# The mixers' list scheduler prices VectorE, ScalarE and GpSimd instructions from a profile

## Chip, cores and metric

One core of a Trainium2 chip. The metric is the device time of one execution in microseconds (us), the median of several runs. Engines: PE is TensorE, DVE VectorE, ACT ScalarE, POOL GpSimd, SP the queue that issues most transfers.

## What is computed

One layer of a diffusion transformer block on 256 latent and 256 context tokens of width 1024: modulation vectors, an input projection, two sequence mixers (a diagonal state space "S5" over both directions and a chunked state space "SSD" over both directions), a gated merge, and a mixture of 32 experts of which each token takes 4.

```python
proj_lat = u_lat @ p['w_in']
s5_l, xbc_l, dt_l, z_l, ga_l, gb_l = jnp.split(proj_lat, IN_SPLITS, axis=-1)
...
ya_l, ya_c = s5_mixer(s5_c, s5_l, p, with_ctx_out)
yb_l, yb_c = ssd_mixer(xbc_c, dt_c, z_c, xbc_l, dt_l, z_l, p, with_ctx_out)
...
merged = (sigmoid(ga) * (ya @ w_branch_a) + sigmoid(gb) * (yb @ w_branch_b)) @ w_out
h_lat = h_lat + g_m * merged
h_lat = h_lat + g_f * moe_ffn(rms_norm(h_lat, norm_ffn_w) * (1 + sc_f) + sh_f, p)
return rms_norm(h_lat, final_norm_w)
```

All weights are float32. The expert weights alone are 32 x 3 matrices of 1024 x 1024, 402.7 MB.

## The kernel before, in words

The program has four stages. A front (modulation vectors, the tokens' norm and their split into a high and a low float32r part, small tables), the mixers, the merge (`glu`, `wa`, `wb`, `wo`, 16 weight tiles or more each, with `column` and `split`), and the experts (`moe`), whose weights stream in 384 tiles of 1 MB (`mw`, issued in `Loads.until`, L1856) into 12 and later 17 buffers. The first 12 of them sit in memory that the mixers' front pools give back (`front.close()` after `mixers()`); they are issued during the merge, and the other 5 buffers come with the experts.

The change touches the mixers alone. `mixers()` does not write its instructions in one fixed order. It has some fifteen Python generators, one for each strand of work, which yield before every step the engine that it needs and what it waits for:

- `gemm`: the input projection. For each block of 512 weights a tile `w` is loaded, ACT casts it to the high part `h`, DVE or POOL subtracts to get the low part (also `h`), and PE multiplies (`mm`). 144 such blocks, four load buffers, two PSUM banks.
- `conv`: five-tap convolution of a column, `cv`: one ACT instruction and four SCALAR_TENSOR_TENSORs on DVE, then a Silu. The last tap frees the PSUM bank for `gemm`.
- `decays`, `prep`, `ssd`: for each of 8 groups the SSD scan. `decays` loads `rt` (16 times, one buffer, freed by the last `yps` product of the decay before), DVE makes `et` from it (8 TENSOR_SCALARs), ACT takes exponentials, POOL multiplies `rt`, and `ssd` multiplies `et` by `xl` (two TENSOR_TENSORs), accumulates `yps` on PE, and ends a group with `mb`, a norm (`zt` squared on ACT, summed on PE, square root `rs` on ACT, reciprocal and `dg` on DVE, spread by PE), and `ybT`.
- `vgen`, `tables`, `states`, `outputs`: the S5 scan. `vgen` makes `V`, `tables` makes `T` on POOL, `states` makes `rot`, `Y` and `l4a`; `outputs` makes 16 weight blocks `Wt` (the generator `gen`), passes each through PE and ACT twice into `strip`, writes four strips to DRAM and reads them back as `Toe` in 2 x 8 transfers.
- `sigmoids`: the last 16 columns of the projection (the gates), which share the two PSUM banks of `gemm`.

`Plan` (L1331 on) then plays a list scheduler: it keeps a clock for each engine, at each step takes the generator that can start first, and among those on the same engine within 260 ns of it the one with the best rank (`PRIO`, `PACE`). A clock is moved by the instruction's price, which `Planned.cost` gives (L1446 on). The prices therefore set the order in which the instructions are written, and with it, after the framework's own placement, the order of each engine's queue. `gemm` also looks at the clocks: a low part goes to DVE where `plan.clock["dve"] + 600 < plan.clock["pool"] + 1200`, else to POOL. Every planned instruction is recorded in one line, L1442, so that the trace is read by tile names.

Of the kernel before, what the change touches and what calls it, by code (L numbers as in the profile page):

```python
# [1407 lines left out]
def key(x):  # L1408
    return getattr(x, "tensor", x).name


class Planned:
# [33 lines left out]
    def cost(self, op, args, kw, out, ins, n):  # L1446
        plan, name = self.plan, self.name
        if name == "pe":
            wide = ins[0]
            m = math.prod(wide.shape[1:])  # L1450
            part = 0.25 if m <= 32 else 0.5 if m <= 64 else 1
            if op == "transpose":
                return 109 * wide.shape[0] / P
            return max(n, 16) * (4 if ins[1].dtype == F32 else 1) * 0.42 * part
        if name == "act":
            f = next((a for a in args if isinstance(a, AF)), None)
            table = plan.SETS.get(f, plan.table)
            switch, plan.table = 1280 * (table != plan.table), table
            return 60 + 0.85 * n + switch
        if name == "pool":  # L1460
            return 80 + 2.2 * n
        if op == "tensor_tensor_scan":
            return 63 + 2.1 * n
        if op == "reciprocal":
            return 63 + 6.3 * n
        fast = op in ("tensor_copy", "tensor_scalar") and not any(key(a) in plan.psum for a in (out, *ins))
        return 63 + (0.52 if fast else 1.05) * n


class Shared:  # L1470
# [476 lines left out]
```

## Time and profile before

| | us |
|---|---|
| runs: median (lowest, highest) | 1853.15 (1849.97, 1854.26) |
| the profiled execution, its own time | 1846.35 |
| its span, first to last instruction | 1844.2 |
| busy in the span: PE, DVE, ACT, POOL | 1589.1, 904.5, 506.8, 290.0 |

The profiled execution has 2.15 us outside its span. Busy time of an engine is an average over stages with different limits, so the stages are read one by one: a view by windows gives each engine's busy time in a stretch; the view of waits says what an engine stood idle for; the timeline lists an engine's instructions with their start, length and, in brackets, the idle time before them and what ended it.

### The profile page before, as it was taken

Reading aid. Unit: us, or ns where it says so; the run is one execution under the profiler, and the core shown is the slowest. Engines: PE = TensorE matmul, PEld = TensorE weight load, DVE = VectorE, ACT = ScalarE, POOL = GpSimd, SP = SyncE. Lnnn points to the kernel's source line nnn. Section 1 sums busy time; section 2 is a strip of 40 time slices with the busy share of each in tenths; the row PEclk is TensorE's granted clock in tenths of the full one; section 3 lists DMA queues with packets and bytes.
Section 4 is the critical chain, followed back from the end, with each engine's and each line's share of the span. In section 5 each row is a group of like instructions: output and inputs, shape, how many; then the busy total and the mean of one; then the engine's idle time right before and its main releaser. Section 6 shows DMA issues by size and latency. Waiting matters only on the chain. (4 is left out here: it accounts for less than half of the span.)

```text
span 1844.2 us, 27968 instructions
## 1 busy us (share of the span) xinstructions
PE 1589.1 (86%) x11118; PEld 935.1 (51%) x11118; DVE 904.5 (49%) x1671; ACT 506.8 (27%) x893; POOL 290.0 (16%) x297
## 2 busy tenths in 40 slices
PE   6798888976988799897998888898888889988987
PEld 3576666764766698783533232333333444333443
DVE  7668899888898546664222222242222223212233
ACT  5333453552435565342111111111111111111111
POOL 5133445435331330100000000000000000000000
PEclk8899898987997999998999999999999999988998
DMA  8677554444542357784999999999998999999984
GB/s 309 181 236 237 178 144 136 119 121 110 148 127 64 114 155 264 235 281 161 417 418 417 417 418 417 413 418 417 418 410 350 418 417 418 418 417 419 418 349 174
DMA packets 141415, 539.36 MB, mean 292 GB/s; under 512 B 31736, under 2 KB 44952, under 8 KB 91920
## 3 DMA queue, kind: packets, MB, share of 16 engines
q1 hardware_dynamic: 136032, 526.95, 75.7%
q10 hardware_dynamic: 4608, 7.95, 1.3%
q8 instruction: 143, 2.34, 0.5%
q0 software_dynamic: 560, 1.52, 0.3%
q14 instruction: 72, 0.59, 0.1%
HBM read 529.60 MB, written 6.77 MB: 291 GB/s over the span
## 5 line engine op out<-in xcount | busy, mean ns | idle before, releaser
L1519 PE MATMUL p_gu<-mw,xe 128*64 128x512 f32 x2048 | 474.8, 601 | 45.2 <-DMA mw<-in_mu 28.4
L1442 PE MATMUL mm<-uh,h 128*128 128x256 f32 (+1 forms) x1152 | 323.6, 361 | 45.2 <-DVE cv L1442 29.9
L1519 PEld LDWEIGHTS p_gu<-mw,xe 128*64 128x64 f32 x2048 | 174.2, 137 | 335.7 <-issue 176.8
L1442 PEld LDWEIGHTS mm<-uh,h 128*128 128x128 f32 x1152 | 209.6, 201 | 85.4 <-issue 42.3
L1629 PE MATMUL p_y<-mw,aT 128*64 128x512 f32 x1024 | 243.4, 627 | 3.4 <-issue 3.4
L1442 PE MATMUL mm<-ul,h 128*128 128x256 f32 (+1 forms) x576 | 202.5, 352 | 0.0
L1442 POOL TENSOR_TENSOR h<-w,h 128x512 fp32r<-128x512 f32 x99 | 150.3, 1522 | 279.3 <-ACT h L1442 213.6
L1637 DVE SCALAR_TENSOR_TENSOR yw<-p_y,gs,xq 64x512 f32<-64x512 f32 x64 | 48.0, 750 | 287.3 <-PE p_y L1629 286.2
L1629 PEld LDWEIGHTS p_y<-mw,aT 128*64 128x64 f32 x1024 | 75.3, 144 | 147.4 <-issue 144.0
L1442 ACT CAST h<-w 128x512 fp32r<-128x512 f32 x144 | 88.1, 618 | 168.7 <-PE mm L1442 121.2
L1442 PEld LDWEIGHTS mm<-ul,h 128*128 128x128 f32 x576 | 116.0, 201 | 13.5 <-issue 3.1
L1533 DVE TENSOR_SCALAR au<-p_gu 128x512 f32<-128x512 f32 x32 | 22.1, 692 | 198.7 <-PE p_gu L1519 198.7
L1639 ACT CAST yh<-yw 64x512 fp32r<-64x512 f32 x64 | 39.4, 616 | 285.4 <-DVE yw L1637 285.4
L1527 DVE TENSOR_SCALAR ag<-p_gu 128x512 f32<-128x512 f32 (+1 forms) x34 | 23.0, 676 | 169.8 <-PE p_gu L1519 169.8
L1442 DVE SCALAR_TENSOR_TENSOR cv<-mm,cw,cv 128x508 f32<-128x508 f32 (+3 forms) x128 | 85.6, 673 | 11.0 <-ACT cv L1442 10.6
L359 DVE TENSOR_TENSOR low<-w,hi 128x512 fp32r<-128x512 f32 x80 | 59.6, 751 | 41.6 <-ACT hi L357 40.3
L1528 ACT ACTIVATE as<-ag 128x512 f32<-128x512 f32 (+1 forms) x34 | 21.0, 617 | 210.5 <-DVE ag L1527 210.5
L1442 ACT ACT_TABLE_LOAD x55 | 70.6, 1283 | 29.9 <-DVE cv L1442 29.1
L357 ACT CAST hi<-w 128x512 fp32r<-128x512 f32 x80 | 49.4, 620 | 70.3 <-PE mm L349 24.8
L1613 PE MATMUL p_t<-ident,au 128*128 128x128 f32 x128 | 30.5, 325 | 39.7 <-PEq L1730 25.2
L1442 DVE TENSOR_SCALAR et<-rt,acs,lnd 128x128 f32<-128x128 f32 x128 | 45.9, 413 | 23.6 <-DMA rt<-acd 23.4
L1442 DVE TENSOR_TENSOR h<-w,h 128x512 fp32r<-128x512 f32 x45 | 39.2, 872 | 31.8 <-ACT h L1442 31.8
(452 smaller groups left out, 2335.2 us busy)
## 6 DMA issues: line engine op xcount, KB each, us to landing
mw<-in_mg SPq DMA_DIRECT2D x128, 1024.0 KB
mw<-in_mu SPq DMA_DIRECT2D x128, 1024.0 KB
mw<-in_md SPq DMA_DIRECT2D x128, 1024.0 KB
w<-in_wg SPq DMA_DIRECT2D x96, 256.0 KB
ada<-in_ada SPq DMA_DIRECT2D x32, 256.0 KB
Toe<-in_ada SPq DMA_DIRECT2D x16, 512.0 KB
vT<-Ed SPq DMA_DIRECT2D x16, 512.0 KB
l8a<-in_ada SPq DMA_DIRECT2D x16, 512.0 KB
```

The source lines that it names most:

```text
L357: act.copy(hi, w)
L359: lo.tensor_tensor(low, w, hi.bitcast(F32), op=ALU.subtract)
L1442: return fn(*args, **kw)
L1519: mm = pe.matmul(dst[c * q:c * q + c, 0:n], lhs(k), w[:, o:o + n], start=(i == 2 and k == 0), stop=(k == KD - 1))
L1527: dve.tensor_scalar(g_, pg, 7.0, None, op0=ALU.min)
L1528: sg = act.activation(s_, g_, AF.Sigmoid, scale=1.702)
L1533: dve.tensor_scalar(u_, pu, -7.0, 7.0, op0=ALU.max, op1=ALU.min)
L1613: pe.transpose(pa[:, q * P:(q + 1) * P], u_[:, q * P:(q + 1) * P], ident)
L1629: self.done = pe.matmul(py[64 * q:64 * q + 64], aT[:, k % 4, k // 4], wts[e, 2, c // load.unit][:, c % load.unit:c % load.unit + 512], sta ...
L1637: dve.scalar_tensor_tensor(w[rows], self.py[rows], self.gs[rows, nh, j:j + 1], gf[rows, 512 * nh:512 * nh + 512], op0=ALU.mult, op1=ALU.mult)
L1639: act.copy(self.hi[rows, nh], w[rows])
```

## The change

New prices in `Planned.cost`: a larger fixed part for all three engines, a larger still one on ScalarE where the scale is a tile, forms of VectorE instruction told apart (TENSOR_SCALAR, SCALAR_TENSOR_TENSOR, the rest), and a factor of 1.2 for other VectorE instructions of which no operand is in PSUM. TensorE's prices, the ranks and all other constants stay.

```diff
@@ -1456,15 +1456,20 @@
             f = next((a for a in args if isinstance(a, AF)), None)
             table = plan.SETS.get(f, plan.table)
             switch, plan.table = 1280 * (table != plan.table), table
-            return 60 + 0.85 * n + switch
+            return (330 if hasattr(kw.get("scale"), "shape") else 150) + 0.89 * n + switch
         if name == "pool":
-            return 80 + 2.2 * n
+            return 300 + 2.3 * n
         if op == "tensor_tensor_scan":
-            return 63 + 2.1 * n
+            return 115 + 2.1 * n
         if op == "reciprocal":
-            return 63 + 6.3 * n
-        fast = op in ("tensor_copy", "tensor_scalar") and not any(key(a) in plan.psum for a in (out, *ins))
-        return 63 + (0.52 if fast else 1.05) * n
+            return 145 + 6.3 * n
+        if op == "tensor_scalar":
+            return 280 + 0.48 * n
+        if op == "scalar_tensor_tensor":
+            return 200 + 1.06 * n
+
+        shared = not any(key(a) in plan.psum for a in (out, *ins))
+        return (145 + 1.04 * n) * (1.2 if shared else 1)
```

The instructions of the mixers stay the same but for two low parts, which go from POOL to DVE (99 and 45 before, 97 and 47 now), and two more table loads on ACT (66, now 68 in the program). Their order moves almost from the mixers' start. Three places of it:

DVE, the end of the second of the eight groups of the SSD scan: `mb`, its product with `zt`, the reciprocal `rs`, `dg` and the first `ybT`. Before, from that product to the reciprocal:

```order
L1442 TENSOR_TENSOR mb<-mb,zt 128x512
L1442 SCALAR_TENSOR_TENSOR strip<-id_551,d_127,strip 128x16
L1442 TENSOR_TENSOR vtv<-V,vT 128x512
L1442 SCALAR_TENSOR_TENSOR cv_2704<-mm,cw,cv_2704 128x2x254
L1442 TENSOR_TENSOR vT<-V,vT 128x4x128
L1442 SCALAR_TENSOR_TENSOR cv_2704<-mm,cw,cv_2704 128x2x255
L1442 TENSOR_TENSOR h<-w,h 128x512
L1442 SCALAR_TENSOR_TENSOR cv_2704<-mm,cw,cv_2704 128x2x255
L1442 RECIPROCAL rs<-rs 128x2
```

Now, from the last `mb` to `ybT`:

```order
L1442 SCALAR_TENSOR_TENSOR mb<-cv_1983,ssdd,yps 128x256
L1442 TENSOR_TENSOR bt<-bt,aux 128x2x256
L1442 TENSOR_TENSOR mb<-mb,zt 128x512
L1442 RECIPROCAL rs<-rs 128x2
L1442 TENSOR_TENSOR dg<-ident,rs 128x256
L1442 TENSOR_TENSOR vtv<-V,vT 128x512
L1442 SCALAR_TENSOR_TENSOR ybT<-mb,ssdn,aux 128x256
```

Work that stood between the product, the reciprocal and `ybT` has gone from there: the reciprocal follows the product at once, and between `dg` and the first `ybT` one instruction is left.

SP, the last strip of S5 (its write to DRAM and its 2 x 8 reads `Toe`) and the last loads of `rt` for the decays. Before:

```order
L1442 DMA rt<-acd 128x1024
L1442 DMA w<-in_wgate 128x512 x5
L1442 DMA strip_5733<-strip 4x128x240
L1442 DMA rt<-acd 128x1024
L1442 DMA w<-in_wgate 128x512
L1442 DMA Toe<-strip_5733 16x8x128 x8
L1442 DMA w<-in_wgate 128x512 x3
L1442 DMA rt<-acd 128x1024
L1442 DMA Toe<-strip_5733 16x8x128 x8
```

Now:

```order
L1442 DMA w<-in_wgate 128x512 x8
L1442 DMA rt<-acd 128x1024 x2
L1442 DMA strip_5810<-strip 4x128x240
L1442 DMA Toe<-strip_5810 16x8x128 x8
L1442 DMA rt<-acd 128x1024
L1442 DMA w<-in_wgate 128x512 x2
L1442 DMA Toe<-strip_5810 16x8x128 x8
```

The last `rt` but one has moved ahead of the strip's write, and the last `rt` stands behind the first eight `Toe`.

DVE, the same end of the mixers: the last strip (TENSOR_TENSOR and SCALAR_TENSOR_TENSOR `strip`) and the last decay but one (`et<-rt` x8 and its products `et<-et,xl`). Before:

```order
L1442 TENSOR_TENSOR h<-w,h 128x512
L1442 TENSOR_TENSOR strip<-strip,w_6188 128x16
L1442 SCALAR_TENSOR_TENSOR strip<-id_551,d_127,strip 128x16
L1442 TENSOR_TENSOR xw_6165<-aux,wend 128x512
L1442 SCALAR_TENSOR_TENSOR mb<-cv_5204,ssdd,yps 128x256
L1442 TENSOR_TENSOR bt<-bt,wend 128x2x256
L1442 SCALAR_TENSOR_TENSOR mb<-cv_5266,ssdd,yps 128x256
L1442 TENSOR_TENSOR bt<-bt,aux 128x2x256
L1442 TENSOR_TENSOR mb<-mb,zt 128x512
L1442 TENSOR_TENSOR h<-w,h 128x512
L1442 TENSOR_SCALAR et<-rt,acs,lnd 128x128 x8
L1442 RECIPROCAL rs<-rs 128x2
```

Now:

```order
L1442 TENSOR_TENSOR mb<-mb,zt 128x512
L1442 TENSOR_TENSOR strip<-strip,w_6359 128x16
L1442 TENSOR_SCALAR et<-rt,acs,lnd 128x128 x8
L1442 SCALAR_TENSOR_TENSOR strip<-id_551,d_127,strip 128x16
L1442 RECIPROCAL rs<-rs 128x2
L1442 TENSOR_TENSOR dg<-ident,rs 128x256
L1442 SCALAR_TENSOR_TENSOR ybT<-mb,ssdn,aux 128x256 x2
L1442 TENSOR_TENSOR et<-et,xl 128x4x128 x2
L1442 TENSOR_TENSOR h<-w,h 128x512 x2
L1442 TENSOR_SCALAR et<-rt,acs,lnd 128x128 x8
```

The last instruction of the last strip now stands behind the eight TENSOR_SCALARs of the last decay but one; before, it stood ahead of them by seven instructions.

## Rows read from the trace of the kernel before

**Rows 1.** The page's 40 slices: share of the DMA engines, and GB/s.
```profile
DMA  8677554444542357784999999999998999999984
GB/s 309 181 236 237 178 144 136 119 121 110 148 127 64 114 155 264 235 281 161 417 418 417 417 418 417 413 418 417 418 410 350 418 417 418 418 417 419 418 349 174
```
**Rows 2.** Issues of the expert weights, from the view of the tile mw.
```profile
L1856 SPq DMA_DIRECT2D mw<-in_mg x128: 327/328/2254, 689.5 to 1776.8; - x128
L1856 SPq DMA_DIRECT2D mw<-in_md x128: 327/328/1332, 787.1 to 1797.7; - x128
```
**Rows 3.** Busy time by windows: us, then PE, PEld, DVE, ACT, POOL, PEclk, DMA, GB/s.
```profile
96.00:606.70 510.70, 430.06 (x4031) 337.38 (x4029) 439.95 (x812) 219.73 (x355) 215.31 (x206) 0.90 0.50 145
606.70:652.20 45.50, 33.69 (x334) 29.03 (x330) 21.31 (x44) 25.37 (x36) 12.49 (x7) 0.89 0.38 110
652.20:684.20 32.00, 32.00 (x294) 31.93 (x293) 11.80 (x17) 20.70 (x39) 14.51 (x12) 1.00 0.62 185
684.20:845.00 160.80, 138.19 (x1054) 130.58 (x1053) 106.60 (x203) 74.91 (x145) 11.51 (x5) 0.95 0.71 238
845.00:1844.00 999.00, 886.13 (x4843) 362.15 (x4840) 257.29 (x410) 121.94 (x235) 2.59 (x2) 0.96 0.96 393
```
**Rows 4.** Waits of DVE from 96 to 606.7 us: total, times, longest.
```profile
DVE cv L1442 <- ACT cv L1442: 10.6, 5, 4.1
DVE strip L1442 <- ACT strip L1442: 9.9, 4, 5.5
DVE et L1442 <- DMA rt<-acd: 9.6, 4, 5.5
DVE rot L1442 <- PE s L1442: 7.4, 4, 2.9
...
DVE ybT L1442 <- PE aux L1442: 1.9, 1, 1.9
```
**Rows 5.** Timeline of DVE, 606 to 652 us: start, length, what, [idle before].
```profile
606.10 0.68 DVE L1442 TENSOR_TENSOR et<-et,xl 128x512 f32<-128x512 f32 x1
...
610.41 0.47 DVE L1442 SCALAR_TENSOR_TENSOR mb<-cv,ssdd,yps 128x256 f32<-128x256 f32 x1
...
620.21 2.14 DVE L1442 TENSOR_SCALAR et<-rt,acs,lnd 128x128 f32<-128x128 f32 x8 [4.81 <-DMA rt<-acd]
...
627.77 3.06 DVE L1442 TENSOR_TENSOR et<-et,xl 128x512 f32<-128x512 f32 x2
...
636.76 2.14 DVE L1442 TENSOR_SCALAR et<-rt,acs,lnd 128x128 f32<-128x128 f32 x8 [5.34 <-DMA rt<-acd]
...
649.85 0.17 DVE L1442 RECIPROCAL rs<-rs 128x2 f32<-128x2 f32 x1 [2.65 <-ACT rs L1442]
...
651.27 0.87 DVE L1442 SCALAR_TENSOR_TENSOR ybT<-mb,ssdn,aux 128x256 f32<-128x256 f32 x2 [0.79 <-PE aux L1442]
```
**Rows 6.** Timeline of SP's queue, 609 to 638 us.
```profile
609.47 0.56 SPq L1442 DMA_DIRECT2D strip<-strip  x1
610.13 2.15 SPq L1442 DMA_DIRECT2D rt<-acd  x1
614.25 0.33 SPq L1442 DMA_DIRECT2D w<-in_wgate  x1
618.97 5.05 SPq L1442 DMA_DIRECT2D Toe<-strip  x8
...
633.03 0.33 SPq L1442 DMA_DIRECT2D rt<-acd  x1
```
**Rows 7.** DVE by line and form, 45 to 652 us: count, busy, mean ns, idle before.
```profile
L1442 DVE TENSOR_TENSOR V<-V,vT 128x512 f32<-128x512 f32 x48 | 42.9, 914 | 0.1
...
L1442 DVE TENSOR_TENSOR et<-et,xl 128x512 f32<-128x512 f32 x32 | 30.5, 972 | 1.6 <-ACT et L1442 1.5
L1442 DVE TENSOR_TENSOR h<-w,h 128x512 fp32r<-128x512 f32 x34 | 30.3, 893 | 14.4 <-ACT h L1442 14.4
```
**Rows 8.** The same instructions as minimum, median and maximum ns.
```profile
L1442 DVE TENSOR_TENSOR V<-V,vT x48: 661/684/2869, 98.0 to 524.5; 128x512 f32<-128x512 f32 x48
```

## The prediction

> **What bounds the kernel now.** I start with the 40 slices [rows 1]. From slice 20 on the DMA engines are full, at 417 or 418 GB/s but for a few slices; before that they are half idle. The full part is the expert weights: 402.7 MB at 418 GB/s are 963 us. Next, when they may start [rows 2]: the first tile is issued at 689.5 us, after the mixers, and the last at 1797.7. Until the experts begin at about 845 us only 12 tiles of 1 MB fit. So the end of the kernel is the end of the mixers plus a stretch that the change does not touch: whatever the mixers lose or gain arrives at the end in full, one to one.
>
> The windows [rows 3] divide the rest. From 96 to 606.7 us, 510.7 us, DVE is busy for 440.0, POOL for 215.3, ACT for 219.7. PE shows 430.1, but its overlapping matmuls are counted with modelled ends and it waits inside its blocks. DVE is the engine that sets the pace there, with 70.7 us idle. The waits [rows 4] split that idle time over many causes, none above 10.6 us. From 606.7 to 652.2 us DVE is busy for 21.3 of 45.5 us: a serial chain, the last two decays [rows 5]. Each waits for its load of `rt`, which waits for the decay before. From 652.2 to 684.2 PE is busy throughout: the gate columns, which cannot be shortened by an order. So the new order can act on 70.7 us of idle in the middle, on the chain of 45.5 us, and on how long DVE's own instructions take.
>
> **The change, part by part.** It adds no work and removes none. A table load more or less on ACT lies beside DVE's work and costs nothing while ACT is busy for 43% of the middle; without that cover the two new ones would cost a few us. Two low parts pass from POOL to DVE at 0.893 us each [rows 7]. What counts is how much DVE work stands ahead of a fixed point: with each form's mean duration, the work up to the products of the 14th decay is 0.8 us more than before. **+0.8 us.**
>
> *The end chain.* Call T0 the end of those products, 606.78 us now [rows 5]. The next `mb`, which waits for the decay's matmuls, starts 3.6 us later; the `rt` load for the 15th decay is issued at T0 + 3.4 [rows 6], but its TENSOR_SCALARs start only at T0 + 13.4. The `rt` load after it takes 3.7 us (633.03 to 636.76, rows 5 and 6). The difference is the strip's write, issued just ahead: `Toe`, which needs it, is not issued until 9.5 us after it [rows 6]. In the new order this `rt` stands ahead of the write, so the data are there at T0 + 7.1, and some 7.5 us of DVE work are written ahead of the TENSOR_SCALARs: they start at T0 + 7.5 and gain 6 us. Then SP takes most of it back. The strip's last DVE instruction follows the TENSOR_SCALARs (2.1 us), so its write is issued at T0 + 9.9; eight `Toe` wait 9.5 us for it and take 5.05 us to issue; only behind them comes the last `rt`, at T0 + 24.4. Now it is issued at T0 + 26.2. From there to the end of the last `ybT` it is 19.1 us (633.03 to 652.14) in both. So the chain ends at T0 + 43.5 instead of 45.4: **-1.9 us**, between -6 (the strip's write is no longer in the way) and +6 (the strip comes 8 us later, when ACT or PE holds it up).
>
> *`rt` in the middle.* 9.6 us in four waits, the longest 5.5 behind another strip [rows 4]. A decay needs 3.4 us of matmuls and 3.7 us of load after the one before, 7.1 in sum. In the new order four of the earlier decays have 6.7 to 8.2 us of DVE work in between, enough or nearly; one still has its load behind a strip. I keep 5.5 us for that one: **-4.1 us**, bounds -9.6 and +5.
>
> *`strip` in the middle.* DVE waits 9.9 us for ACT's copies [rows 4], 5.5 at once. Between the last `Wt` of a block and its `strip` the new order leaves less than 5 us once before T0 (before: twice), so the short ones are hardly fewer; but the longest wait had 30 us of DVE work in between and came from PE's queue standing still. Such an accident may go or come again. I take **-4 us**, bounds -9.9 and +5.
>
> *The end of a group.* This speaks against the change. The reciprocal needs ACT's square, PE's sum and ACT's root; at the very end, with nothing in between, that wait is 2.65 us, and `ybT` then waits 0.79 [rows 5]. In the middle there is so far one wait, 1.9 us for `ybT` [rows 4], because other work stands in between. In the new order the second group has none before the reciprocal, and of the first six groups one has nothing and four have one instruction between `dg` and `ybT`. With a latency of 1.35 us, half way between 0.79 and 1.9, and 0.68 us for one instruction: 1.35 + 4 x 0.7 + 2.65 - 1.9 = **+4.9 us**, bounds 0 and +19 (the last group's 3.44 us in six groups, less 1.9).
>
> *Sum:* 0.8 - 1.9 - 4.1 - 4.0 + 4.9 = -4.3 us. Against the profiled execution, 1846.35 us, that is 1842.0. That execution is 6.8 us faster than the median of the runs, 1853.15, against which the changed kernel will be read: 1848.9.
>
> *What the new prices assume, against the row.* The change multiplies all VectorE instructions without a PSUM operand by 1.2. The rows do not show a factor: `V` has a median of 684 ns and a maximum of 2869 [rows 8], with a mean of 914 [rows 7]; most instances are not stretched at all. The Trainium skill ("SBUF — State Buffer", Who interferes with whom) says that GpSimd and a VectorE instruction with two SBUF inputs exclude each other for a whole instruction and do not share; by that rule, the trace agrees, no constant factor can be right for any one instruction, and the stretch depends on which two instructions meet. Over the median of 684 ns, `V`, `et<-et` and `h` lose 48 x 0.230 + 32 x 0.288 + 34 x 0.209 = 27.3 us [rows 7]. In the sum I leave this unchanged, because POOL does the same work less two low parts.
>
> **Rivals.**
> 1. *The other waits fall too.* Of the 70.7 us idle, 21.4 are in the three terms above (9.6, 9.9, 1.9); 49.3 are for `cv`, `rot` and others [rows 4]. The prices are nearer to the rows than before (a `V` was priced 600 ns, now 813), so a consumer should less often be written ahead of its data. If these fall by the 40% that I took for `rt` and `strip`, that is another -19.7: 1829 us. Against it: PE's prices, whose queue caused the longest waits, are unchanged.
> 2. *The waits only change places.* The order moves, the idle time stays near 70 us; this is also the case in which the prices hardly act because the framework places the instructions. 1853 us. The DVE orders differ from the first S5 block on, which speaks against the second half.
> 3. *The end of the groups decides.* If each of six groups waits like the last one now, 3.44 us, the term is +18.7 instead of +4.9: 1848.9 + 13.8 = 1862.7. The other terms give -9.2; the kernel becomes slower than before once a group waits (9.2 + 1.9) / 6 = 1.85 us on average. For it: PE works through its queue in order and may be inside a block of the projection. Against it: but for the second, the groups before the seventh keep three to seven rows between product and reciprocal.
> 4. *More meetings of DVE and POOL.* If the stretch of 27.3 us grows by a third, +9: 1858 us. A third less is as easily had, since the order decides who meets whom; I give the growth the chance because nothing in the change avoids a meeting. The Trainium skill ("SBUF — State Buffer", Who interferes with whom) has issue order decide which of the two blocks, which fits both signs.
>
> **Numbers.** Forecast 1848.9 us, chance 0.36, with 1842 to 1856 as its own range. Rival 1: 0.22. Rival 2: 0.14. Rival 3: 0.16. Rival 4: 0.12. 0.2% is 3.7 us, about what a measurement can tell from no change. Faster by more than that: rival 1 and somewhat over half of the forecast's range, 0.22 + 0.22 = 0.44. The same: the rest of the forecast but 0.02, rival 2 and a little of rival 4, 0.12 + 0.14 + 0.02 = 0.28. Slower: 0.16 + 0.10 + 0.02 = 0.28. The range from 1832 to 1863 leaves out half of rival 1, the far end of rival 3, and little else.
>
> **What would show it.** In the profile after, the first weight tile should be issued some 4 us before 689.5 us less any offset at the start, and the experts' stretch should be as long as now. DVE's `rt` wait before the 15th decay should be near zero and that before the 16th remain at 5 us or more; the strip's write should be issued after that decay's TENSOR_SCALARs. The waits of `rs` and `ybT` in the middle should be near 7 us in sum. I am wrong in kind if the experts' stretch takes up or gives back what the mixers did, if DVE's busy time moves by more than 5 us at equal work (then the meetings with POOL decide), or if DVE waits mostly for PE's queue in places that I have not named.

## The result, and the profile after

The changed kernel is slower: 1901.8 us (1897.4 to 1905.8, 4 runs) against 1853.4 for the kernel before, a ratio of 1.027 [1.024, 1.030], some 48 us. The forecast was 1848.9, with a range from 1832 to 1863. The profiled execution took 1902.17 us, with a span of 1900.1. It lies at the median of its runs, while that of the kernel before lies some 7 us under its median, so the two spans differ by 55.9 us where the medians differ by 48.

The view by windows, as [rows 3]. Its first two cuts are at the same events (the end of the products of the 14th decay, 657.96, and the last `ybT`, 707.6); the third is at the first expert tile, 742.9, where [rows 3] cut 5.3 us ahead of that tile. Columns us, PE, PEld, DVE, ACT, POOL, PEclk, DMA, GB/s:

```profile
96.00:657.96 561.96, 442.03 (x4036) 349.46 (x4038) 438.76 (x811) 230.51 (x365) 222.60 (x207) 0.87 0.47 135
657.96:707.60 49.64, 36.84 (x340) 31.62 (x337) 25.96 (x48) 20.10 (x31) 12.24 (x6) 0.69 0.30 85
707.60:742.90 35.30, 35.30 (x331) 34.82 (x331) 13.23 (x23) 22.92 (x43) 13.20 (x11) 1.00 0.52 165
742.90:900.00 157.10, 131.12 (x1006) 123.36 (x1005) 102.58 (x194) 71.28 (x137) 11.50 (x5) 0.96 0.72 239
900.00:1899.00 999.00, 884.67 (x4846) 357.87 (x4843) 257.59 (x411) 122.23 (x236) 2.58 (x2) 0.96 0.96 393
```

The first weights of the tile `mw`, as in [rows 2]:

```profile
L1861 SPq DMA_DIRECT2D mw<-in_mg x128: 327/328/2058, 742.9 to 1832.7; - x128
```

The experts' last 999 us have the same DMA share as before, 0.96, and the same 393 GB/s. The first tile is issued 53.4 us later (689.5 to 742.9), and from there to the end of the span it is 2.5 us more (1154.7, now 1157.2). So the loss arose in the mixers: 51.2 us up to T0, the end of the products of the 14th decay (606.78 before, 657.96 now), 4.3 in the end chain, and 2.1 less from the last `ybT` to the first tile. The windows of DVE up to T0 say what kind of time it is. The kernel before and then the changed one; columns as above, DVE alone:

```profile
45.00:606.78 561.78, 476.04 (x889) 0.89 0.51 148
```
```profile
45.00:657.96 612.96, 477.31 (x894) 0.87 0.48 140
```

The same work, 1.3 us more of it, and 50 us more idle time (561.78 - 476.04 = 85.7; 612.96 - 477.31 = 135.7). The waits of DVE from 96 us to T0, as [rows 4] (total, times, longest):

```profile
DVE strip L1442 <- ACT strip L1442: 19.1, 3, 12.4
DVE xl L1442 <- PE aux L1442: 13.1, 6, 2.7
DVE h L1442 <- ACT h L1442: 12.3, 5, 9.5
DVE et L1442 <- DMA rt<-acd: 11.0, 3, 8.6
DVE et L1442 <- ACT et L1442: 9.8, 1, 9.8
DVE mb L1442 <- PE yps L1442: 9.5, 2, 9.3
DVE rot L1442 <- PE s L1442: 8.0, 3, 4.4
...
DVE ybT L1442 <- PE aux L1442: 5.6, 6, 2.2
...
DVE rs L1442 <- ACT rs L1442: 2.9, 1, 2.9
DVE cv L1442 <- ACT cv L1442: 2.0, 3, 1.3
```

Four of these kinds, which [rows 4] do not show, in the kernel before:

```profile
DVE h L1442 <- ACT h L1442: 6.4, 4, 4.8
...
DVE xl L1442 <- PE aux L1442: 3.0, 4, 1.6
...
DVE mb L1442 <- PE yps L1442: 2.1, 2, 1.7
...
DVE et L1442 <- ACT et L1442: 0.4, 1, 0.4
```

No one wait took the place of another: most kinds are longer, of those shown only `cv` is clearly shorter, and four single waits (12.4, 9.8, 9.5, 9.3) hold 41 us. Summed over the whole view by the engine that ended them, DVE's waits for PE rose from 24.3 to 49.4 us, those for ACT from 29.2 to 47.5, and those for transfers from 15.6 to 23.7.

One of the four, read on three engines. PE's timeline of the changed kernel from 407 us, then DVE's and POOL's (start, length, what, [idle before]):

```profile
407.12 1.22 PE L1442 MATMUL mm<-uh,h 128*128 128x512 f32 x2 [4.34 <-POOL h L1442]
408.14 0.63 PE L1442 MATMUL mm<-ul,h 128*128 128x512 f32 x1
...
409.42 0.63 PE L1442 MATMUL mm<-ul,h 128*128 128x512 f32 x1
...
412.72 0.39 PE L1442 MATMUL mm<-ul,h 128*128 128x512 f32 x1
...
413.42 0.40 PE L1442 MATMUL mm<-ul,h 128*128 128x512 f32 x1
...
417.47 0.66 PE L1442 MATMUL w<-Wt,Bb 64*32 64x128 f32 x16
```
```profile
399.23 0.68 DVE L1442 TENSOR_TENSOR vtw<-EP,Ct 128x512 f32<-128x512 f32 x1
399.84 0.68 DVE L1442 TENSOR_TENSOR V<-V,vtv 128x512 f32<-128x512 f32 x1
...
406.16 1.45 DVE L1442 TENSOR_TENSOR h<-w,h 128x512 fp32r<-128x512 f32 x1 [0.22 <-ACT h L1442]
420.03 0.17 DVE L1442 TENSOR_TENSOR strip<-strip,w 128x16 f32<-128x16 f32 x1 [12.42 <-ACT strip L1442]
```
```profile
398.75 9.99 POOL L1442 TENSOR_TENSOR h<-w,h 128x512 fp32r<-128x512 f32 x2 [1.52 <-ACT h L1442]
```

DVE's next instruction needs `w`, and `w` stands in PE's queue behind a block of the projection that waits 4.3 us for its low part and then runs for 10.3 us. DVE had its work done at 407.6 and stood still until 420.0.

The low part is late for a reason of its own. The first of the two in POOL's row took 8.3 us, the longest of all 97 (minimum, median and maximum ns):

```profile
L1442 POOL TENSOR_TENSOR h<-w,h x97: 1260/1308/8311, 86.2 to 734.4; 128x512 fp32r<-128x512 f32 x97
```

While it ran, DVE worked without a gap until 405.9; whether that held it back, no run isolates. At the median it would have been ready before PE asked for it. An estimate from these rows: the wait of 4.3 us, and 2.2 that PE's clock then cost (last section), would have gone, and some 5.9 of DVE's 12.4 us would have stayed, for the place of the block ahead of `w`.

### The profile page after: what moved, and what is told of

Its sections match the earlier page's. It is cut to its first block, busy times and chain, and to the rows that moved or that the text cites. A ratio compares the mean times of both kernels' runs of the same rounds, so it can differ in the third digit from the quotient of the medians.

```text
span 1900.1 us, 27962 instructions
## 1 busy us (share of the span) xinstructions
PE 1596.2 (84%) x11118; PEld 942.0 (50%) x11118; DVE 906.3 (48%) x1673; ACT 511.1 (27%) x895; POOL 295.0 (16%) x295
## 3 DMA queue, kind: packets, MB, share of 16 engines
q0 software_dynamic: 560, 1.52, 0.2%
## 5 line engine op out<-in xcount | busy, mean ns | idle before, releaser
L1442 PEld LDWEIGHTS mm<-uh,h 128*128 128x128 f32 x1152 | 213.7, 205 | 81.3 <-issue 26.2
L1442 POOL TENSOR_TENSOR h<-w,h 128x512 fp32r<-128x512 f32 x97 | 158.4, 1640 | 327.4 <-ACT h L1442 247.7
L1442 ACT ACT_TABLE_LOAD x57 | 73.1, 1283 | 51.2 <-DVE cv L1442 49.5
L357 ACT CAST hi<-w 128x512 fp32r<-128x512 f32 x80 | 49.5, 620 | 72.2 <-PE mm L349 18.4
L1619 ACT COPY aT<-p_t 128x256 f32<-128x256 f32 x64 | 23.8, 373 | 114.5 <-PE p_t L1618 114.4
```

The lines of the kernel that those rows point to most:

```text
L357: act.copy(hi, w)
L1442: return fn(*args, **kw)
L1619: act.copy(aT[:, 2 * h:2 * h + 2].rearrange("p a b s -> p (a b s)"), pa[:, 256 * h:256 * h + 256])
```

## Experiments

All ratios are against runs of the kernel before on the same chip. "Sums" are the plan's own prices, added up over the mixers for DVE and for PE in us: arithmetic on the program, no times of the chip. Idle is the time in which DVE was not busy from 96 us to the first `mw`: the width of that window less its busy time. The first `mw` and the idle time are those of the profiled execution; that of the kernel before is 4 to 7 us faster than its medians.

| run | sums DVE : PE | median us | ratio, interval | first `mw` | DVE idle |
|---|---|---|---|---|---|
| before | 373 : 392 = 0.95 | 1851 to 1853 | 1 | 689.5 | 116.3 |
| changed | 521 : 392 = 1.33 | 1901.8 | 1.027 [1.024, 1.030] | 742.9 | 168.9 |
| e_pool | 382 : 392 = 0.97 | 1857.6 | 1.003 [1.001, 1.005] | 702.4 | 122.0 |
| e_dve | 516 : 392 = 1.31 | 1906.5 | 1.030 [1.026, 1.034] | 745.9 | 179.1 |
| e_act | 374 : 392 = 0.95 | 1843.6 | 0.997 [0.995, 0.999] | 677.0 | 94.2 |
| n1_dve_plus3 | 374 : 392 = 0.95 | 1869.6 | 1.011 [1.008, 1.015] | 702.8 | 122.1 |
| n2_pool_plus5 | 371 : 392 = 0.94 | 1872.1 | 1.010 [1.007, 1.013] | 705.0 | 131.2 |
| a_pe130 | 520 : 510 = 1.02 | 1889.1 | 1.021 [1.018, 1.023] | 722.8 | 145.2 |
| a_dve072 | 382 : 392 = 0.97 | 1861.4 | 1.005 [1.003, 1.007] | 701.3 | 118.4 |
| b_dve140 | 512 : 392 = 1.30 | 1906.9 | 1.030 [1.028, 1.032] | 750.7 | 169.9 |
| a_unit133 | 519 : 522 = 0.99 | 1883.3 | 1.015 [1.012, 1.018] | 718.7 | 138.7 |
| b_dve120 | 445 : 392 = 1.14 | 1891.7 | 1.021 [1.019, 1.024] | 728.3 | 149.4 |
| a1_dve_plus3 | 526 : 392 = 1.34 | 1912.7 | 1.033 [1.029, 1.036] | 756.2 | 178.2 |
| b_pe075 | 380 : 294 = 1.29 | 1899.9 | 1.025 [1.021, 1.028] | 732.6 | 153.5 |
| a_pe150 | 516 : 589 = 0.88 | 1867.6 | 1.009 [1.006, 1.012] | 704.1 | 121.7 |
| b_dve085 | 321 : 392 = 0.82 | 1863.9 | 1.009 [1.005, 1.012] | 703.7 | 121.4 |
| ea_pe115 | 376 : 451 = 0.83 | 1874.7 | 1.013 [1.010, 1.016] | 704.5 | 132.8 |
| b_v_late | 373 : 392 = 0.95 | 1873.2 | 1.014 [1.011, 1.016] | 713.5 | 128.2 |
| a_v_early | 525 : 392 = 1.34 | 1906.8 | 1.029 [1.027, 1.031] | 754.0 | 185.8 |
| e_act_again | 374 : 392 = 0.95 | 1847.5 | 0.998 [0.9960, 0.9997] | 679.9 | 98.0 |

### Which engine's prices

Each engine's new prices alone in the kernel before (e_dve has the lines of the change's diff from `tensor_tensor_scan` on, and no others), and a disturbance of 3 ns.

```diff
@@ e_pool @@
-            return 80 + 2.2 * n
+            return 300 + 2.3 * n
@@ e_act @@
-            return 60 + 0.85 * n + switch
+            return (330 if hasattr(kw.get("scale"), "shape") else 150) + 0.89 * n + switch
@@ n1_dve_plus3 @@
-        return 63 + (0.52 if fast else 1.05) * n
+        return 66 + (0.52 if fast else 1.05) * n
```

> Only GpSimd's price is the new one (300 + 2.3n in place of 80 + 2.2n); VectorE and ScalarE keep the old prices. Theory A (GpSimd's price alone does it: the products of a decay's rt are queued on POOL between the products of the tables, PE waits for them inside its queue, and everything behind waits too): 1885 to 1905 us, with waits of PE for rt from POOL of over 10 us in sum, as in the changed kernel (19.1). Theory B (VectorE's prices do it): 1850 to 1860 us, those PE waits under 2 us as before the change (0.8). Theory C (any disturbance of the prices gives another order and another sum of waits; the constants that steer the order fit the old prices only by trial): anything from 1850 to 1900, with waits in other places than in the changed kernel.

> Only VectorE's prices are the new ones; ScalarE and GpSimd keep the old. Theory A (GpSimd's price does it): 1850 to 1860 us, PE's waits for rt from POOL under 2 us. Theory B (VectorE's prices do it): 1885 to 1905 us, DVE idle in the mixers some 50 us more than before the change. Theory C (any disturbance reorders): anything from 1850 to 1900, and the sum of the three single steps is not the step of the whole.

> Only ScalarE's prices are the new ones (150 or 330 + 0.89n in place of 60 + 0.85n). Theories A and B (another engine's price does it): 1849 to 1858 us. Theory C (any disturbance reorders): 1850 to 1900, most likely 10 to 30 us slower than before the change.

> The prices of before the change, but the fixed part of VectorE's common price is 66 ns in place of 63: no better and no worse as a price. Theories A and B (the wrongness or the size of a new price does it): within 0.3% of before, 1849 to 1858 us. Theory C (the list scheduler turns any small disturbance into another order, and the order before the change is a picked one): a thousand rows move on DVE, and the time rises by 5 to 40 us.

VectorE's prices alone give the whole loss, 1906.5. GpSimd's cost some 5 us, ScalarE's gain some 5. Theory A had a good-looking row behind it: in the changed kernel PE waits 18.4 us for `rt` from POOL from 96 to 658 us, which it did not before.

```profile
PE yps L1442 <- POOL rt L1442: 18.4, 3, 8.8
```

With GpSimd's price alone it is

```profile
PE yps L1442 <- POOL rt L1442: 1.3, 2, 0.7
```

and with VectorE's prices alone it is 10.4 us. So GpSimd's price does not make that wait; it is one place where a bad order shows. The disturbance says something else: 3 ns on a price of 600, which makes no price better or worse, cost 1.1%. The order before looks like a good draw, and a part of what a change of prices costs is leaving it; n2_pool_plus5 below, a second such disturbance, cost 1.0%.

### Size or relation of VectorE's prices

One line scales a price. It stands here as in a_pe130, on the changed kernel; a_dve072 has `(0.715 if name == "dve" else 1)` there, and b_dve140 `(1.4 if name == "dve" else 1)` on the kernel before.

```diff
-                cost = self.cost(op, args, kw, out, ins, n)
+                cost = self.cost(op, args, kw, out, ins, n) * (1.3 if name == "pe" else 1)
@@ n2_pool_plus5 @@
-            return 80 + 2.2 * n
+            return 85 + 2.2 * n
```

> The changed kernel with TensorE's prices in the plan times 1.3. The plan's own sums for the mixers: before, PE 392 and DVE 373 us of 481; changed, PE 392 and DVE 521 of 606, so that PE is thought to be idle for 35%; here PE 510 and DVE 521 of 618. Theory D (the ratio: VectorE's prices went up by 40% and TensorE's stayed, so the plan writes consumers right behind PE's products and DVE waits): most of the loss returns, 1850 to 1870 us, and DVE's waits in the mixers fall from 157 to some 110 us. Theory C (any disturbance reorders, the order before is a picked one): 1860 to 1910 with no preference. Theory F (the relation of VectorE's forms to each other): 1890 to 1910 as changed.

> The changed kernel with VectorE's new prices all times 0.715: the new relation of the forms, but the old sum (DVE 382 us in the plan, before 373, changed 521). Theory D (the ratio of VectorE to TensorE): most of the loss returns, 1850 to 1870 us. Theory F (the relation of the forms to each other, a TENSOR_SCALAR at 341 in place of 130 ns above all): 1890 to 1910. Theory C: 1855 to 1900 with no preference.

> The kernel before with VectorE's old prices all times 1.4: the old relation of the forms, the new sum (DVE 512 us in the plan). Theory D (the ratio): 1890 to 1910 us, as with VectorE's new prices alone (1906.5). Theory F (the relation of the forms): 1845 to 1865. Theory C: 1855 to 1900 with no preference.

> The prices of before, but GpSimd's fixed part is 85 ns in place of 80: a second small disturbance, which moves some 900 rows on DVE. Theory C (the order before is a picked one): 5 to 40 us slower, as the first small disturbance (1869.6). Theory D (the ratio, which this leaves as it is): within 20 us of before on either side, and far from 1900.

The old prices times 1.4 are as bad as the new ones (1906.9 and 1906.5), and the new ones times 0.715 nearly as good as the old (1861.4). So it is the size of VectorE's prices; which form costs what matters little. Theory F falls. Against TensorE's price, though, Theory D got only 13 us back.

The next scale TensorE by 1.33 in the changed kernel, with the fixed times below (a_unit133), and VectorE by 1.2 in the kernel before (b_dve120); a1_dve_plus3 disturbs the changed kernel.

```diff
@@ a_unit133 @@
-NEAR = 260
+NEAR = 350
...
-ISSUE = 60
+ISSUE = 80
...
-                plan.clock["dma"] = max(plan.clock["dma"], start + 500) + max(math.prod(out.shape) * 4 / 360, 450)
-                end = plan.clock["dma"] + 1600
+                plan.clock["dma"] = max(plan.clock["dma"], start + 670) + max(math.prod(out.shape) * 4 / 270, 600)
+                end = plan.clock["dma"] + 2150
...
-                end += 60
+                end += 80
...
@@ a1_dve_plus3 @@
-        return (145 + 1.04 * n) * (1.2 if shared else 1)
+        return (148 + 1.04 * n) * (1.2 if shared else 1)
```

> The changed kernel with everything that the change left as it was raised in proportion: TensorE's prices times 1.33, a transfer's 500 + bytes/360 + 1600 to 670 + bytes/270 + 2150 ns, the hand-over between engines from 60 to 80, the issue from 60 to 80, the window in which steps compete from 260 to 350. In the plan DVE is then 521 of some 655 us busy. Theory D2 (the change raised VectorE's prices against every other time in the plan, transfers and hand-overs too; raising TensorE alone mends one part, 1889): 1855 to 1875 us, the last scan of the S5 branch starts near 560 to 580 us (before 532, changed 624), and DVE's waits for transfers fall from 60 us, as measured with VectorE's prices alone, to 30. Theory H (steps of the S5 branch lose against the projection and the convolution whenever DVE has several to choose from, which a higher price of DVE makes more frequent whatever the rest costs): 1880 to 1905, the last scan after 600 us. Theory C (any disturbance reorders): 1855 to 1900 with no preference.

> The kernel before with VectorE's old prices times 1.2: between before (times 1: 1851) and times 1.4 (1906.9). Theories D2 and H (the scale of VectorE's prices decides, step by step): 1870 to 1890 us, and the last scan of the S5 branch between the 532 us of before and the 640 of times 1.4. Theory C (any disturbance gives the same spread): 1855 to 1875, as the two small disturbances (1869.6 and 1872.1).

> The changed kernel with VectorE's common fixed part at 148 ns in place of 145, as small a disturbance as the one tried around before. Theories D2 and H (the scale decides, and a small disturbance moves the time by 20 us at most): 1882 to 1920 us. Theory C (the spread is all there is, and the changed kernel was an unlucky draw): about 1865, the middle of the disturbed kernels around before.

Step by step: times 1 is 1851, times 1.2 is 1892, times 1.4 is 1907. The changed kernel was no unlucky draw (1912.7 with 3 ns more), so Theory C is not all there is. Raising everything in proportion gave back 18 us, less than Theory D2 said.

### Against TensorE, from the other side

The line above with `(0.75 if name == "pe" else 1)` on the kernel before, `(1.5 if name == "pe" else 1)` on the changed one, `(0.85 if name == "dve" else 1)` on the kernel before, and `(1.15 if name == "pe" else 1)` on e_act.

> The kernel before with TensorE's prices times 0.75 and nothing else: all prices that the change touches are the old ones. In the plan DVE is 380 us and PE 294, a ratio of 1.29, as in the changed kernel (521 to 392, 1.33); before it is 373 to 392, 0.95. Theory D (the ratio decides, whichever side of it is moved): 1885 to 1910 us, the last scan of the S5 branch after 590 us (before 532, changed 624). Rival (VectorE's prices by their size, against transfers and hand-overs or against reality): 1850 to 1870 us, the last scan at 525 to 550.

> The changed kernel with TensorE's prices times 1.5: DVE 516, PE 589 in the plan, a ratio of 0.88. Theory D (the ratio decides): 1850 to 1875 us, and the last scan before 560 us. Rival (VectorE's size by itself): 1880 to 1900, as with times 1.3 (1889).

> The kernel before with VectorE's old prices times 0.85: the ratio 0.81. Theory D, if lower is always better: 1830 to 1850 us. If the kernel before sits at a picked optimum of its constants (Theory C): 1855 to 1880.

> ScalarE's new prices alone (1843.6 us) and TensorE's times 1.15: the ratio 0.83. Theory D, if lower is always better: 1825 to 1845 us. Theory C (a picked optimum, and 20 us for any disturbance): 1855 to 1880.

This decides between the ratio and the size of VectorE's prices by itself. With all the prices that the change touches at their old values, a cheaper TensorE alone costs 2.5%, nearly what the change costs; with all of them at the new values, a TensorE at 1.5 brings back 34 of 48 us. The windows from 96 us to the first `mw`, of the kernel before, the changed one, b_pe075 and a_pe150:

```profile
96.00:689.50 593.50, 501.05 (x4695) 403.65 (x4694) 477.23 (x879) 269.18 (x435) 242.31 (x225) 0.90 0.50 144
```
```profile
96.00:742.90 646.90, 514.17 (x4698) 415.90 (x4697) 477.95 (x880) 273.53 (x437) 248.05 (x223) 0.86 0.46 133
```
```profile
96.00:732.60 636.60, 501.95 (x4707) 408.46 (x4706) 483.14 (x890) 264.54 (x430) 221.55 (x213) 0.88 0.46 135
```
```profile
96.00:704.10 608.10, 502.73 (x4697) 404.09 (x4697) 486.41 (x876) 265.55 (x432) 252.16 (x229) 0.91 0.50 141
```

PE and DVE do the same work within 3% in all four; the windows differ by 53 us. Sorted by the ratio of the sums, the runs with prices changed fall in groups: 0.82 to 0.97, 1844 to 1875 us; 0.99 and 1.02, 1883 and 1889; 1.14, 1892; 1.29 to 1.34, 1900 to 1913. Below 0.97 a lower ratio gains nothing more (1863.9 and 1874.7).

### Is the late S5 branch the reason?

In the slow kernels one strand is plainly late. The scans of the S5 branch, before and with VectorE's new prices alone (min/median/max, first and last start):

```profile
L1442 DVE TENSOR_TENSOR_SCAN Y<-R,Y x8: 2259/2279/3308, 172.6 to 534.4; 128x1024 f32<-128x1024 f32 x8
```
```profile
L1442 DVE TENSOR_TENSOR_SCAN Y<-R,Y x8: 2259/2282/3373, 196.7 to 637.8; 128x1024 f32<-128x1024 f32 x8
```

Only the ranks are changed for the next two; e_act_again is e_act once more.

```diff
@@ b_v_late: PRIO of the kernel before @@
-..., vgen=-0.2, states=-0.5, ...
+..., vgen=0.8, states=0.5, ...
@@ a_v_early: PRIO of the changed kernel @@
-..., vgen=-0.2, states=-0.5, ...
+..., vgen=-0.7, states=-1, ...
```

> The kernel before with all its old prices; only the ranks of the S5 branch are lowered by 1 (vgen -0.2 to 0.8, states -0.5 to 0.5), so that its steps lose more often on DVE. Theory L (the late S5 branch makes the time): the last scan near 610 to 640 us and 1890 to 1910. Rival (the lateness only goes with it; DVE's idle time comes from everywhere): the last scan late, but 1850 to 1875.

> The changed kernel with the ranks of the S5 branch raised by 0.5 (vgen -0.7, states -1), all its prices kept. Theory L: the last scan 40 to 80 us earlier than 624, and the time 1860 to 1885. Rival: the last scan earlier, the convolution and the decays later in exchange, and 1895 to 1930.

> ScalarE's new prices alone, as before (1843.6 us, 0.3% faster), with more runs. If that was real: 1840 to 1847 us and an interval below 1. If it was chance: the interval holds 1.

Theory L falls both ways. With the last scan as late as in the changed kernel (626), the kernel before loses 22 us, about what a disturbance of 3 ns costs (19); with the last scan 67 us earlier than in the changed kernel (559 in place of 626), that kernel stays at 1906.8. The lateness goes with the loss and does not by itself make it. ScalarE's new prices alone are faster than the kernel before by 0.3% and, measured again, by 0.2% [0.9960, 0.9997].

## Why the prediction was wrong

**What held.** That the loss or gain of the mixers arrives in full at the end; that no work is added (1.3 us of DVE up to T0, forecast 0.8); that the stretch of `V` by POOL stays as it is. For the last, the tile `V` after, as [rows 8]:

```profile
L1442 DVE TENSOR_TENSOR V<-V,vT x48: 675/684/2880, 98.3 to 613.2; 128x512 f32<-128x512 f32 x48
```

DVE's busy time from 96 us to the first `mw` is 477.2 before and 478.0 after, so rival 4 cost nothing on DVE. It looked there alone: on POOL a low part took up to 8.3 us (up to 5.1 before), with a mean of 1.64 us in place of 1.52.

**The end chain** was read rightly in its order and wrongly in its lengths.

```profile
656.67 1.29 DVE L1442 TENSOR_TENSOR et<-et,xl 128x512 f32<-128x512 f32 x2
...
668.08 2.14 DVE L1442 TENSOR_SCALAR et<-rt,acs,lnd 128x128 f32<-128x128 f32 x8
...
689.73 2.14 DVE L1442 TENSOR_SCALAR et<-rt,acs,lnd 128x128 f32<-128x128 f32 x8 [3.29 <-DMA rt<-acd]
...
704.11 0.17 DVE L1442 RECIPROCAL rs<-rs 128x2 f32<-128x2 f32 x1 [3.95 <-ACT rs L1442]
...
706.73 0.87 DVE L1442 SCALAR_TENSOR_TENSOR ybT<-mb,ssdn,aux 128x256 f32<-128x256 f32 x2 [1.29 <-PE aux L1442]
```
```profile
670.46 0.56 SPq L1442 DMA_DIRECT2D strip<-strip  x1
679.65 5.30 SPq L1442 DMA_DIRECT2D Toe<-strip  x8
685.07 0.52 SPq L1442 DMA_DIRECT2D rt<-acd  x1
```

(DVE, then SP, of the changed kernel.) The 15th decay no longer waits for its load; its TENSOR_SCALARs start at T0 + 10.1, forecast 7.5; the strip's write follows at T0 + 12.5, forecast 9.9; the eight `Toe` wait 9.2 us for it, and the last `rt` leaves at T0 + 27.1, forecast 24.4. From there to the last `ybT` it is 22.5 us and not 19.1. T0 + 49.6 in place of T0 + 43.5: +4.3 against the kernel before, forecast -1.9 and inside its bounds. DVE's wait for the last `rt` is 3.3 us, where 5 or more were forecast.

**The waits in the middle** carry the error. `rt` was forecast at 5.5 us and is 11.0, `strip` at 5.9 and is 19.1, `rs` and `ybT` at 6.8 and are 8.5. And the 49.3 us of other waits, which the sum left as they were and rival 1 had falling, rose: `xl` from 3.0 to 13.1, `mb` from 2.1 to 9.5, `et` for ACT from 0.4 to 9.8, `h` from 6.4 to 12.3, while `cv` fell from 10.6 to 2.0; all that is not in the three terms came to some 85 us. So rival 1 has the wrong sign, rival 2 the wrong sum (the idle time up to T0 rose by 50 us), and rival 3 is a small part: its waits rose by 6.6 us, to 1.4 per group, under the 1.85 from which they alone would have decided.

**The step that failed** is the sentence that the prices "are nearer to the rows than before", so that "a consumer should less often be written ahead of its data", and beside it the `strip` term, whose bound of +5 took the distances along DVE's queue for cover (it rose by 9.2). I held each price against its own row and never added them up. The sums say that the plan before had DVE at 373 us and PE at 392, a ratio of 0.95; busy over the mixers, from 96 us to the first `mw`, were 477.2 and 501.1 (the first of the four windows above), which is 0.95 too. The change takes DVE to 521 and leaves PE at 392, so the plan takes PE to be idle for a third of its time, while on the chip the two read 478.0 and 514.2. The runs above show what this ratio is worth: moved by TensorE's price alone, it costs the kernel before 49 us (b_pe075) and gives the changed one 34 back (a_pe150). I had named the reservation ("PE's prices ... are unchanged") and used it only to doubt a gain.

What I take to happen between the sums and the idle time is argued from the stall at 407 us, not shown: a plan with dear DVE steps and cheap matmuls believes that a block of the projection, put ahead of `w`, is over before DVE has done its dozen instructions, and on the chip DVE is done first. Of that stall this would explain, by the estimate above, 5.9 of 12.4 us; the rest came from the late low part and the clock.

**What the prices were taken from.** The timeline above shows two TENSOR_TENSORs of 0.68 us that start 0.61 us apart; the eight TENSOR_SCALARs at 668.08 take 2.14 us together, 0.27 each, where the mean duration of one was 413 ns in the kernel before. Durations overlap: from 45 to 652 us of the kernel before the counts times the means of all 931 DVE instructions give 560 us, and DVE was busy for 497. The Trainium skill ("Perfetto Trace Analysis", Optimizing Scalar/DVE Operations) says so: the engine is busy for about half of the overhead that an instruction's latency shows, since the write's acknowledgement runs beside the next instruction; the rows agree, with 0.68 us long and 0.61 apart. The old price of this TENSOR_TENSOR, 601 ns, is the distance of starts; the new one, 145 + 1.04 x 512 = 677, is the duration, and 813 with the factor of 1.2. Of a TENSOR_SCALAR the old price, 130 ns, was half the distance.

**What stays open.** a_pe130 and a_unit133 bring the ratio to 1.02 and 0.99 and remain at 1889 and 1883. Whether this is the 20 us of a disturbed order on top of a ratio still 4 to 7% above the old one, or the ranks, which suit a plan that has PE as the scarce engine, was not told apart. Nor was it tried to choose new ranks for the new prices beyond a_v_early.

## To carry to other kernels

When a planner's prices are changed for some engines, add up the plan's prices by engine, before and after, and hold the ratio of the sums against the busy times of a window; a price that is right for one engine alone can be wrong for the order. Take an engine's price from the distance between starts of instructions that did not wait, not from durations; no run here tried such prices. And before a difference is put down to a cause, disturb the planner by something that means nothing: here 3 ns moved the time by 1.1%, so that one changed kernel tells apart only what is larger.

## What the hardware showed unasked

PE pays for a wait twice. In the timeline above it works at one step of three matmuls per 0.70 us (412.72 to 413.42), but after the wait of 4.34 us at one per 1.28 us (408.14 to 409.42). PE's windows in that stretch (us, PE, PEclk, DMA, GB/s):

```profile
398.00:402.60 4.60, 4.60 (x27) 1.00 0.17 57
402.60:407.10 4.50, 0.18 (x1) 0.80 0.00 0
407.10:411.90 4.80, 4.78 (x11) 0.50 0.74 209
411.90:417.40 5.50, 5.50 (x24) 0.98 0.46 151
```

The granted clock falls while PE stands and is 0.50, its lower level of 1.2 GHz, for the next 4.8 us. Eleven matmuls at 0.70 / 3 would have been 2.6 us: the wait of 4.3 us cost 2.2 more, and DVE, waiting behind this block, paid both. In the end chain, from 658 to 707.6 us, the clock is 0.69; in the same chain of the kernel before it was 0.89 [rows 3]. What share of the loss this is, the runs do not separate from the waits.
